# An encoder layer: head 0 of the dilated attention prepared beside two dense groups instead of one, and three loads of output weights tied to later heads

## The chip, the cores and the metric

The kernel runs on one core of a Trainium2 chip. The metric is the device time of one execution in microseconds (us). Five engines matter here: TensorE (PE, matrix products; PEld is its weight load), VectorE (DVE), ScalarE (ACT), GpSimd (POOL) and SyncE (SP), which issues most DMAs. Each works through its own queue in order, and they wait for each other by semaphores.

## The reference, cut to what matters

One encoder layer over 1024 positions of width 1024, in float32:

```
proj = rms_norm(x) @ w_in                       # qA kA vA qB kB vB
out_a = dense attention, 8 query heads on 2 key/value heads, QK-norm and axial rotary
out_b = 8 heads: three dilated windows (128,1), (512,4), (2048,16), ALiBi distance penalty,
        merged by their softmax denominators
x = x + concat(rms_norm(out_a), rms_norm(out_b)) @ w_out
x = x + (gelu(gate) * value) @ w_down           # gate, value: depthwise conv of rms_norm(x) @ w_up
```

## The kernel before

The program is one straight sequence of instructions. Its stages are the input projection, the dense attention, the dilated attention, the output projection, the up-projection with convolution and gate, and the down-projection. All large operands live in two arenas on chip, `bigf` (plain float32) and `bigr` (operands of products), addressed by fixed offsets, so that buffers of different stages share places. PSUM (`ps`) is used as eight banks of 512 columns. Most products are made of three: a value is split into a rounded copy (an ACT copy) and the rest (a DVE or POOL subtraction), and high*high, high*low and low*high are added.

**Order.** The Python code issues the steps in program order, but a scheduler then orders each engine's queue by the data dependences; an instruction whose operands are free early can be put well ahead of where the code has it. Lists of small steps (`prep`) are taken a few at a time between the steps of the main loops, by `take`.

**Dense attention** (loop from L1037): 16 groups `g`, each four query heads of one block of 128 queries. `a_main` runs over 8 key tiles `kt`: two score products (L624, L625) into bank 2 or 3, an exponential on ACT (L627), and two tiles later the product with the values (`pv`, L619, four matmuls of 65 columns). After each tile it takes `plan[kt]` steps of `prep`. `a_prep(g + 1)` has seven: `nat` (split of the queries), `first` (four transposes, copy L592), four `mx` (score products L597 and a row maximum L598), `last` (transposes, copy L605). With the plan (1, 1, 1, 1, 1, 1, 1, 0) group g prepares group g + 1. Group 15 has no successor. It takes the 16 steps for head 0 of the dilated attention instead, by the plan (3, 2, 2, 2, 2, 2, 2, 1).

**Dilated attention** (loop from L1077): 8 heads `h`, each 8 steps `s`. `b_s` makes a bias product (L747), score products (L759 and L761 for s < 4, L769 and L770 behind), and an exponential (L773). For s < 4 the result is then split (ACT copy L775, DVE subtraction L776), for the others it is multiplied by a count on DVE (L778). Two steps later `b_pv` multiplies with the values (L790, L795) and collects in `F_OS` (L798 on ACT, L802 on DVE); `b_out` transposes back (L807) and normalises (L639, L640). While a head runs, the next one is prepared: `b_split` (copies L675 and L576, subtractions on POOL) and the 15 steps of `b_prep`:

- `trq`: four transposes (L177) and the ACT copy L700; `trk`: four transposes, ACT copies L691 and L692, DVE casts L693 and L694;
- `mx`, eight times: products into banks 0 and 1 (L707, L708, L711, L712), each followed by a DVE row maximum (L718);
- `trl`: a DVE maximum (L726), four transposes, ACT copy L731, whose result the scores L761 need.

In the same list stands `b_split(h + 1)`, so head 1 is split inside the preparation of head 0.

**Output weights.** `w_out` is loaded in eight parts of 512 KB (`wo_load`, L812) and split (`wo_split`: ACT L818, DVE L819). A table gives the head and step after which each is issued:

```
wo_early = {(4, 0): [(wo_load, 0)], (4, 5): [(wo_split, 0), (wo_load, 1)], (5, 5): [(wo_split, 1), (wo_load, 2)], ...
F_WOR = [O_F + o for o in (2560, 2560, 2560, 3584, 5632, 6656, 2560, 5632)]
```

Parts 0, 1 and 2 go through the same place, where the dense attention keeps its values until its last group. Nothing in the data ties load 0 to head 4. Parts 5 to 7 are split behind the last head.

Of the kernel before, what the change touches and what calls it, by code (L numbers as in the profile page):

```python
# [83 lines left out]
F_OS = O_F + 1536  # L84
# [14 lines left out]
F_WOR = [O_F + o for o in (2560, 2560, 2560, 3584, 5632, 6656, 2560, 5632)]  # L99
# [24 lines left out]
def tile_encoder_layer(ctx, tc, x, w_in, gains, outg, norm1_g, norm2_g, w_out, w_up, conv_w, conv_b,  # L124
# [15 lines left out]
    vec = nc.vector  # L140
# [4 lines left out]
    def f(off, n):  # L145
        return bigf[:, off:off + n]
# [62 lines left out]
    def qab(tt):  # L209
        return O_QAB + 1024 * tt  # L210
# [362 lines left out]
    def q_nat(src, stride, eng, n, o, qln=R_QLN):  # L573

        q = fp(src, [stride, n], [1, 64])
        act(rp(R_QD + o, [128, n], [64, 2], [1, 64]), fp(src, [stride, n], [0, 2], [1, 64]), AF.Copy)  # L576
        eng.tensor_tensor(rp(qln + o, [128, n], [1, 64]), q, rfp(R_QD + o, [128, n], [1, 64]), op=OP.subtract)


    def a_prep(g):  # L580
        b, kv = divmod(g, 2)
        q2 = R_Q2A + 512 * (g % 2)
        ql = R_QLA + 512 * (g % 2)

        def nat():
            q_nat(qab(b) + 256 * kv, 64, vec, 4, 512 * kv)

        def first():
            t = next_tr()
            for i in range(4):  # L590
                tr_r(t, i, r(R_QD + 128 * (4 * kv + i), 128))
            act(r(q2, 512), bank(t), AF.Copy)  # L592

        def mx(i):
            for hf in range(2):
                b = hf
                mm(bank(b), r(q2 + 128 * i, 128), r(R_K2A + 1024 * kv + 512 * hf, 512), start=True, stop=True)  # L597
                vec.tensor_reduce(f(SM_MC + 8 * hf + i, 1), bank(b), axis=AX.X, op=OP.max)  # L598

        def last():  # L600
            vec.tensor_tensor(rp(R_QLN + 512 * kv + 64, [128, 4]), f(SM_MC, 4), f(SM_MC + 8, 4), op=OP.max)
            t = next_tr()
            for i in range(4):
                tr_r(t, i, r(R_QLN + 128 * (4 * kv + i), 128))
            act(r(ql, 512), bank(t), AF.Copy)  # L605

        return [nat, first] + [lambda i=i: mx(i) for i in range(4)] + [last]

    def a_main(g, prep, tail, late, plan, late_plan):

        b, kv = divmod(g, 2)
        q2 = R_Q2A + 512 * (g % 2)
        ql = R_QLA + 512 * (g % 2)
        ob = 6 + g % 2
        slots = {}

        def pv(kt):
            for i in range(4):
                mm(bank(ob, 65, 66 * i), f(slots[kt] + 128 * i, 128), f(F_VA + 132 * kt + 66 * kv, 65),  # L619
                   start=(kt == 0 and i == 0), stop=(kt == 7), skip_group_check=True)  # L620

        for kt in range(8):
            st = 2 + kt % 2
            mm(bank(st), r(R_K2A + 1024 * kv + 128 * kt, 128), r(q2, 512), start=True, stop=False)  # L624
            mm(bank(st), r(R_KHA + 1024 * kv + 128 * kt, 128), r(ql, 512), start=False, stop=True)  # L625
            slots[kt] = p_slots()[0]
            act(f(slots[kt], 512), bank(st), AF.Exp)  # L627
            take(prep, plan[kt])
            take(late, late_plan[kt])
            if tail and kt in (0, 1, 2):  # L630
                tail.pop(0)()
            if kt >= 2:
                pv(kt - 2)

        return [lambda: pv(6), lambda: pv(7), lambda: o_norm(ob, 66, qab(b) + 256 * kv, ([64, 4], [1, 64]))]
# [37 lines left out]
    def b_split(h):  # L673
        k3 = fp(F_KN[h % 2], [64, 8], [1, 64])
        act(rp(R_KN, [128, 8], [1, 64]), k3, AF.Copy)  # L675
        gp.tensor_tensor(rp(R_KN + 64, [128, 8], [1, 64]), k3, rfp(R_KN, [128, 8], [1, 64]), op=OP.subtract)
        q_nat(O_QAB + 512 + 64 * h, 1024, gp, 8, 0, R_QLB[h % 2])
        if h < 6:
            load_k(h + 2)

    def b_prep(h):
        k2n, k2c, khn, khc, q2c, qlc = sets(h)

        def trk(hf):

            t = next_tr()
            for i in range(4):
                tr_r(t, i, r(R_KN + 128 * (4 * hf + i), 128))
            nat = pp(512 * t, [256, 2], [32, 8], [1, 32])
            to = lambda o: rp(o + 64 * hf, [32, 2], [128, 8], [1, 32])  # L690
            act(r(k2c + 512 * hf, 512), bank(t), AF.Copy)  # L691
            act(to(k2n), nat, AF.Copy)  # L692
            vec.tensor_copy(r(khc + 512 * hf, 512)[0:64], bank(t)[0:64])  # L693
            vec.tensor_copy(to(khn)[0:64], nat[0:64])  # L694

        def trq(hf):
            t = next_tr()
            for i in range(4):
                tr_r(t, i, r(R_QD + 128 * (4 * hf + i), 128))
            act(r(q2c + 512 * hf, 512), bank(t), AF.Copy)  # L700

        def mx(tt):
            rr, c = divmod(tt, 2)
            q = r(q2c + 128 * tt, 128)
            m0 = k2c + 112 * c
            if rr % 3:
                mm(bank(0, 144 * rr), q, rp(m0, [256, rr], [1, 144]), start=True, stop=True)  # L707
                mm(bank(0, 432 - 144 * rr, 144 * rr), q, rp(m0 + 256 * (rr + 1), [256, 3 - rr], [1, 144]),  # L708
                   start=True, stop=True)
            else:  # L710
                mm(bank(0, 432), q, rp(m0 + (256 if rr == 0 else 0), [256, 3], [1, 144]), start=True, stop=True)  # L711
            mm(bank(1, 256), q, r(k2c + 256 * rr, 256), start=True, stop=True)  # L712
            tmx = F_TMX[h % 2]
            for i, (ps, tab, n) in enumerate((
                    (bank(0, 432), fp(tmx + 384 + 160 * (3 - rr) + 16 * (1 - c), [160, 3], [1, 144]), 432),
                    (bank(1, 256), f(tmx + 128 * (1 - c), 256), 256))):
                junk = f(F_JK2[i], n // 2).bitcast(BF)
                vec.tensor_tensor_reduce(out=heads(junk, 3) if i == 0 else junk, in0=heads(ps, 3) if i == 0 else ps,  # L718
                                         in1=tab, scale=1.0, scalar=-3e38, op0=OP.add, op1=OP.max,
                                         accum_out=f(SM_MC + 8 * i + tt, 1))  # L720
            if tt == 7 and h < 6:
                load_tmx(h + 2)

        def trl(hf):
            qln = R_QLB[h % 2]
            vec.tensor_tensor(rp(qln + 64 + 512 * hf, [128, 4]), f(SM_MC + 4 * hf, 4), f(SM_MC + 8 + 4 * hf, 4),  # L726
                              op=OP.max)
            t = next_tr()
            for i in range(4):
                tr_r(t, i, r(qln + 128 * (4 * hf + i), 128))  # L730
            act(r(qlc + 512 * hf, 512), bank(t), AF.Copy)  # L731

        L = lambda fn, a: (lambda: fn(a))
        return [L(trq, 0), L(trk, 0), L(trk, 1), L(mx, 0), L(trq, 1), L(mx, 1), L(mx, 2),
                L(mx, 3), L(trl, 0), L(mx, 4), L(mx, 5),
                L(b_split, h + 1) if h < 7 else None, L(mx, 6), L(mx, 7), L(trl, 1)]
# [199 lines left out]
    prep = [lambda: fill(rp(R_QLN + 64, [128, 8], [1, 64]), 8, 64, 0.0)] + a_prep(0)  # L936
# [90 lines left out]
    late = last_sums + [t for d in deferred[:2] for t in done(*d, 0)[3:]]  # L1027
# [6 lines left out]
    load_tabs(1)  # L1034

    tail = []
    for g in range(16):  # L1037
        prep = a_prep(g + 1) if g < 15 else [lambda: b_split(0)] + b_prep(0)
        tail = a_main(g, prep, tail, late, (3, 2, 2, 2, 2, 2, 2, 1) if g == 15 else (1, 1, 1, 1, 1, 1, 1, 0),
                      (0, 1, 1, 0, 1, 0, 1, 0) if g < 3 else (0, 0, 1, 0, 1, 0, 1, 0) if g < 7 else (0, 1, 0, 0, 0, 1, 0, 0))  # L1040
        if g == 7:
            dma(f(F_CNT, 384), cnt)
            gp.memset(fp(F_VCN + 64, [66, 8]), 1.0)
            load_vc(0)
        if g == 11:
            load_k(0)
            load_k(1)
        if g == 5:
            v_split(R_VB, F_VBN)
            load_v(1)  # L1050
        take(fills, 1)
# [8 lines left out]

    def mixer_out_early(h, s):
        for fn, k in wo_early.get((h, s), []):
            fn(k)
        if h != 7:
            return
        if s in (0, 2):
            mix_tr(s // 2, 0)
        if s in (1, 3):
            mix_sq(s // 2, 0)
        if s == 4:  # L1070
            dma(f(F_G2, 1024), bcast(norm2_g, 1024))
        if s == 7:
            proj_out(0, 0, 0)
            proj_out(0, 0, 1)

    lag = 2
    for gs in range(64 + lag + 1):  # L1077
        h, s = divmod(gs, 8)
        if s == 0:
            prep = b_prep(h + 1) if h < 7 else []  # L1080
# [375 lines left out]
```

## Time and profile before

| | |
|---|---|
| median of 3 runs | 1342.73 us (1342.39 to 1345.34) |
| profiled execution | 1343.92 us, its span 1342.2 us |
| mean granted TensorE clock | 0.999 |
| ACT busy, DVE busy, POOL busy | 674.0, 991.7, 363.4 us |
| dense groups, PE | first score product at 211.5, last value product at 431.3 us |
| head 0, first bias product | 431.3 us |
| last bias product of head 7 | 590.5 us |
| w_out loads issued | 431.57, 437.99, 449.64, 554.71 us, four more from 573.09 to 582.04 |

All times inside the execution are counted from the start of the span. A row of the order of time gives start, duration, engine, line and operation, and in brackets how long the engine idled before it and whose end released it. L-numbers are lines of the kernel before.

### The profile page before, as it was taken

How to read it: one execution, taken by the hardware profiler on the slowest of the kernel's cores; microseconds unless marked ns; L12 is line 12 of the kernel's file. 1: busy time of each engine (PE TensorE's matmuls, PEld its weight loads, DVE VectorE, ACT ScalarE, POOL GpSimd, SP SyncE). 2: the span in 40 equal slices, each digit the busy share in tenths (PEclk: the TensorE clock that was granted, in tenths of full speed). 3: DMA queues.
4: the chain of work that ended last, by engine and by line, in shares of the span. 5: the costliest groups of instructions: out<-in, count | busy, mean ns of one | idle time of the engine just before them, and what ended most of it. 6: DMA issues, size and time to landing. Idle time of an engine off the chain costs nothing.

```text
span 1342.2 us, 20068 instructions
## 1 busy us (share of the span) xinstructions
PE 1311.1 (98%) x7559; PEld 1134.9 (85%) x7559; DVE 991.7 (74%) x1613; ACT 674.0 (50%) x1057; POOL 363.4 (27%) x274
## 2 busy tenths in 40 slices
PE   8999999999999999999999999999999999999998
PEld 7999989989998888878877788888888888888887
DVE  4987696864545888876579877887787789586664
ACT  7855553644445776764365444444444445244331
POOL 1611123020001222100114565556656651100000
PEclk9999999999999999999999999999999999999999
DMA  7144212000001333252222233232233325897873
GB/s 256 53 123 114 80 39 65 9 9 0 1 1 34 107 105 81 67 166 79 94 87 71 102 110 111 86 102 96 102 115 105 102 101 190 283 311 228 293 223 113
DMA packets 119859, 148.08 MB, mean 110 GB/s; under 512 B 50833, under 2 KB 76881, under 8 KB 119761
## 3 DMA queue, kind: packets, MB, share of 16 engines
q1 hardware_dynamic: 118609, 143.65, 33.3%
q0 software_dynamic: 1152, 3.15, 0.9%
q8 instruction: 59, 0.97, 0.3%
q14 instruction: 39, 0.32, 0.1%
HBM read 112.95 MB, written 33.82 MB: 109 GB/s over the span
## 4 chain that ended last, share of the span: by engine, by line
PE 70%; DVE 16%; ACT 5%; issue 4%; POOL 4%; DMA 1%; SPq 0%; DVEq 0%; ACTq 0%; POOLq 0%
PE ps L619 7%; PE ps L1161 7%; PE ps L1162 7%; PE ps L1163 7%; PE ps L1277 5%; PE ps L1276 5%; PE ps L1278 5%; DVE bigf L1194 4%; PE ps L624 2%; PE ps L597 2%; PE ps L625 2%; POOL bigf L1208 2%; PE ps L862 2%; PE ps L795 2%; PE ps L864 2%
## 5 line engine op out<-in xcount | busy, mean ns | idle before, releaser
L1161 PE MATMUL ps<-bigr 128*128 128x512 f32 x616 | 241.1, 392 | 6.6 <-DVE bigf L1165 6.1
L1162 PE MATMUL ps<-bigr 128*128 128x512 f32 x616 | 239.8, 389 | 0.0
L1163 PE MATMUL ps<-bigr 128*128 128x512 f32 x616 | 239.7, 389 | 0.0
L1144 ACT ACTIVATE bigr<-bigf 128x512 fp32r<-128x512 f32 x154 | 92.8, 624 | 159.2 <-POOL bigf L1136 95.4
L1194 DVE SCALAR_TENSOR_TENSOR bigf<-bigf 128x768 f32<-128x768 f32 (+1 forms) x176 | 146.4, 889 | 26.3 <-ACT bigf L1192 26.3
L619 PEld LDWEIGHTS ps<-bigf 128*128 128x128 f32 x1024 | 139.4, 191 | 10.5
L1161 PEld LDWEIGHTS ps<-bigr 128*128 128x128 f32 x616 | 115.6, 188 | 35.6 <-DVE bigf L1165 9.9
L1145 DVE TENSOR_TENSOR bigr<-bigf,bigr 128x512 fp32r<-128x512 f32 x112 | 116.5, 1057 | 32.6 <-ACT bigr L1144 32.6
L1256 ACT ACTIVATE bigr<-bigf 128x1024 fp32r<-128x1024 f32 x77 | 80.6, 1059 | 119.5 <-PE ps L1278 76.9
L1163 PEld LDWEIGHTS ps<-bigr 128*128 128x128 f32 x616 | 115.6, 188 | 24.2
L1162 PEld LDWEIGHTS ps<-bigr 128*128 128x128 f32 x616 | 115.6, 188 | 23.6
L619 PE MATMUL ps<-bigf 128*128 128x65 f32 x1024 | 134.3, 267 | 0.0
L405 PE MATMUL ps<-bigr 128*128 128x256 f32 x448 | 127.2, 284 | 1.2 <-ACT bigf L291 1.2
L406 PE MATMUL ps<-bigr 128*128 128x256 f32 x448 | 126.8, 283 | 0.0
L407 PE MATMUL ps<-bigr 128*128 128x256 f32 x448 | 126.7, 283 | 0.0
L627 ACT ACTIVATE bigf<-ps 128x512 f32<-128x512 f32 x128 | 75.7, 597 | 93.5 <-PE ps L625 91.1
L1277 PE MATMUL ps<-bigr 128*128 128x512 f32 x308 | 119.9, 389 | 0.0
L1278 PE MATMUL ps<-bigr 128*128 128x512 f32 x308 | 119.8, 389 | 0.0
L1276 PE MATMUL ps<-bigr 128*128 128x512 f32 x308 | 119.8, 389 | 0.0
L1257 DVE TENSOR_TENSOR bigr<-bigf,bigr 128x1024 fp32r<-128x1024 f32 x77 | 93.0, 1221 | 28.7 <-ACT bigr L1256 26.7
L598 DVE TENSOR_REDUCE bigf<-ps 128x1 f32<-128x512 f32 x128 | 86.0, 689 | 23.6 <-PE ps L597 22.2
L1208 POOL TENSOR_TENSOR bigf<-bigf 128x512 f32<-128x512 f32 x44 | 69.1, 1590 | 89.9 <-DVE bigf L1199 65.6
(221 smaller groups left out, 2892.6 us busy)
## 6 DMA issues: line engine op xcount, KB each, us to landing
bigf<-w_down SPq DMA_DIRECT2D x99, 256.0 KB, 4.3
bigf<-w_up SPq DMA_DIRECT2D x44, 512.0 KB, 4.2
bigf<-gscr SPq DMA_DIRECT2D x77, 256.0 KB, 4.1
gscr<-bigf SPq DMA_DIRECT2D x33, 512.0 KB, 2.7
bigf<-w_in SPq DMA_DIRECT2D x8, 1024.0 KB, 5.3
bigf<-x SPq DMA_DIRECT2D x15, 512.0 KB, 6.6
bigf<-tmx SPq DMA_DIRECT2D x8, 672.0 KB, 5.1
bigf<-w_out SPq DMA_DIRECT2D x8, 512.0 KB, 4.0
```

Source lines behind the costliest of these rows:

```text
L405: mm(o, ah, wh, start=(k == 0 and t % 2 == 0 and n != 2), stop=False, skip_group_check=True)
L406: mm(o, ah, wl, start=False, stop=False, skip_group_check=True)
L407: mm(o, al, wh, start=False, stop=(k == 3), skip_group_check=True)
L619: mm(bank(ob, 65, 66 * i), f(slots[kt] + 128 * i, 128), f(F_VA + 132 * kt + 66 * kv, 65), start=(kt == 0 and i == 0), stop=(kt == 7), skip ...
L1145: (gp if n in (2, 4) and m > 3 else vec).tensor_tensor(rp(o + 512, [128, 4], [1, 128]), src, rfp(o, [128, 4], [1, 128]), op=OP.subtract)
L1161: mm(bank(b), wh, th, start=(k == 0 and n in (1, 5, 6, 7)), stop=False, skip_group_check=True)
L1162: mm(bank(b), wh, tl, start=False, stop=False, skip_group_check=True)
L1163: mm(bank(b), wl, th, start=False, stop=(k == 3), skip_group_check=True)
L1194: vec.scalar_tensor_tensor(f(a + o, n), f(i + d, n), w_, f(a + o, n), op0=OP.mult, op1=OP.add)
L1276: mm(o, ah, r(d, 512), start=(q == 0 and n in (1, 5, 2)), stop=False, skip_group_check=True)
L1277: mm(o, ah, r(d + 1024, 512), start=False, stop=False, skip_group_check=True)
L1278: mm(o, al, r(d, 512), start=False, stop=(q == NQ - 1), skip_group_check=True)
```

## The change

The list `prep` now lives across groups. Group 14 gets the steps of `a_prep(15)` and, behind them, those of head 0; it takes 11 steps by the plan (1, 1, 1, 1, 1, 2, 2, 2), so the last four (`b_split(0)`, `trq(0)`, both `trk`) are of head 0. Group 15 takes the other 12 by (2, 2, 2, 2, 1, 1, 1, 1). And for heads below 6 (loads 0, 1 and 2) a DVE copy of one column from `F_OS` into the first column of the load's place is put ahead of the load. `F_OS` is written by the head before, so the copy, and the load that overwrites it, can't be ordered ahead of that.

```
     tail = []
+    prep = []
     for g in range(16):
-        prep = a_prep(g + 1) if g < 15 else [lambda: b_split(0)] + b_prep(0)
-        tail = a_main(g, prep, tail, late, (3, 2, 2, 2, 2, 2, 2, 1) if g == 15 else (1, 1, 1, 1, 1, 1, 1, 0),
+        prep += a_prep(g + 1) if g < 15 else []
+        if g == 14:
+            prep += [lambda: b_split(0)] + b_prep(0)
+        tail = a_main(g, prep, tail, late, {14: (1, 1, 1, 1, 1, 2, 2, 2), 15: (2, 2, 2, 2, 1, 1, 1, 1)}.get(
+            g, (1, 1, 1, 1, 1, 1, 1, 0)),
...
         for fn, k in wo_early.get((h, s), []):
+            if fn is wo_load and h < 6:
+                vec.tensor_copy(f(F_WOR[k], 1), f(F_OS, 1))
             fn(k)
```

## The prediction

> **What bounds the kernel now.** I read the page's busy times first, then the busy time of each engine in stretches of one dilated head, then the order of time of single engines around the change.
>
> ```profile
> PE 1311.1 (98%) x7559; PEld 1134.9 (85%) x7559; DVE 991.7 (74%) x1613; ACT 674.0 (50%) x1057; POOL 363.4 (27%) x274
> ```
>
> The stretches give, after their bounds and length, busy time and (instructions) of each engine, then the granted clock and the DMA columns.
>
> ```profile
> core 0: us, PE busy (x) PEld busy (x) DVE busy (x) ACT busy (x) POOL busy (x), PEclk, DMA share, GB/s
> 391.40:404.80 13.40, 13.40 (x97) 12.30 (x97) 6.15 (x12) 6.29 (x11) 0.00 (x0) 1.00 0.00 1
> 431.30:451.50 20.20, 17.18 (x117) 15.43 (x116) 16.39 (x49) 15.08 (x26) 2.81 (x3) 0.92 0.39 111
> 491.50:511.50 20.00, 19.51 (x141) 16.95 (x139) 17.09 (x54) 13.72 (x25) 3.74 (x4) 1.00 0.37 94
> 511.50:531.80 20.30, 20.00 (x142) 17.01 (x141) 16.47 (x51) 13.73 (x25) 4.98 (x5) 1.00 0.31 81
> 552.20:572.40 20.20, 19.90 (x142) 16.92 (x140) 16.27 (x51) 14.31 (x25) 1.83 (x3) 1.00 0.27 72
> ```
>
> TensorE (PE) is busy for 98% of the span, so a change gains only what PE now idles or runs slowly. A dense group (the 391.40 row) leaves it no idle time, and the later dilated heads leave 0.3 to 0.5 us in 20. Head 0 is the exception: 3.0 us of 20.2 idle, and a mean granted clock of 0.92. PE's own order of time says where (start, duration, instruction; in brackets the idle time before it and what ended it):
>
> ```profile
> 432.10 0.46 PE L177 MATMUL ps<-bigr 128*128 128x128 f32 x4
> 432.40 0.48 PE L747 MATMUL ps<-bigr 128*128 128x512 f32 x1
> 432.71 0.28 PE L759 MATMUL ps<-bigr 128*128 128x256 f32 x1
> 433.34 0.84 PE L177 MATMUL ps<-bigr 128*128 128x128 f32 x8 [0.35 <-ACT bigr L700]
> 435.02 0.39 PE L761 MATMUL ps<-bigr 128*128 128x256 f32 x1 [0.84 <-ACT bigr L731]
> ...
> 437.55 0.73 PE L711 MATMUL ps<-bigr 128*128 128x432 f32 x1 [1.19 <-ACT bigr L691]
> ...
> 439.56 0.41 PE L761 MATMUL ps<-bigr 128*128 128x256 f32 x1
> ...
> 441.68 0.48 PE L747 MATMUL ps<-bigr 128*128 128x256 f32 x2
> 442.00 0.28 PE L759 MATMUL ps<-bigr 128*128 128x256 f32 x1
> ...
> 446.64 0.37 PE L707 MATMUL ps<-bigr 128*128 128x288 f32 x1 [0.62 <-DVE bigf L718]
> ```
>
> The brackets add to 0.35 + 0.84 + 1.19 + 0.62 = 3.0 us, three of the four waits being for ScalarE (ACT). Behind the third, the same product takes 0.41 us instead of 0.28. Two stretches show why:
>
> ```profile
> 433.00:437.40 4.40, 2.18 (x18) 1.87 (x18) 2.22 (x5) 3.71 (x8) 0.00 (x0) 1.00 0.80 249
> 437.40:440.80 3.40, 3.25 (x12) 2.99 (x13) 3.23 (x6) 2.94 (x7) 1.23 (x1) 0.50 0.48 151
> ```
>
> After a stretch in which PE was busy 2.18 of 4.40 us, the granted clock is 0.50 for 3.4 us. The 3.25 us of work there would have taken half at full clock: 1.6 us lost. So the place holds 3.0 + 1.6 = **4.6 us** in all, and no more can be gained.
>
> **The change part by part.** What ACT and VectorE (DVE) did in that place:
>
> ```profile
> 433.89 0.60 ACT L691 ACTIVATE bigr<-ps 128x512 fp32r<-128x512 f32 x1 [0.69 <-PE ps L177]
> 434.38 0.59 ACT L731 ACTIVATE bigr<-ps 128x512 fp32r<-128x512 f32 x1
> 434.86 0.60 ACT L692 ACTIVATE bigr<-ps 128x512 fp32r<-128x512 f32 x1
> 435.33 1.16 ACT L818 ACTIVATE bigr<-bigf 128x1024 fp32r<-128x1024 f32 x1
> 436.38 0.61 ACT L773 ACTIVATE ps<-ps 128x512 f32<-128x512 f32 x1
> 436.89 0.61 ACT L691 ACTIVATE bigr<-ps 128x512 fp32r<-128x512 f32 x1
> ```
> ```profile
> 436.70 1.27 DVE L819 SCALAR_TENSOR_TENSOR bigr<-bigf,bigr 128x1024 fp32r<-128x1024 f32 x1
> 438.01 0.69 DVE L776 TENSOR_TENSOR bigr<-ps,bigr 128x512 fp32r<-128x512 f32 x1
> 438.62 0.67 DVE L693 CAST bigr<-ps 64x512 fp32r<-64x512 f32 x1
> 439.22 0.67 DVE L694 CAST bigr<-ps 64x512 fp32r<-64x512 f32 x1
> ```
>
> The copy L731, on which head 0's first scores wait (the 0.84), stands behind a copy L691 of head 1. The first split of output weights (L818 on ACT, 1.05 us to the next start; L819 on DVE, 1.27) stands ahead of the first exponential L773 and the second L691, and L711 waits 1.19 us for that L691.
>
> *Preparation spread over groups 14 and 15.* The steps are the same 15, and with group 15's own seven and the split of head 0 they make 23 calls: 11 in group 14, 12 in group 15. Nothing is added. In the built program most of the row-maximum products of head 0 stand one key tile of group 15 earlier; its last four transposes now stand ahead of the first scores that use them, and L731 ahead of L700 and L691. In group 14's last tile four copies of 0.48 us stand on ACT between two exponentials, so one comes about 2.5 us after the last instead of the usual 1.7 (13.40 for eight tiles). Worked along PE's new order, that is hidden behind the eight transposes and the value products but for about 0.1 us: **+0.1** (from 0 to 0.8, the whole lateness).
>
> *Loads held back.* Before, SyncE's queue had w_out load 0 ahead of other loads:
>
> ```profile
> 431.57 0.35 SPq L812 DMA_DIRECT2D bigf<-w_out  x1
> 432.94 0.35 SPq L660 DMA_DIRECT2D bigf<-tmx  x1
> ```
>
> Load 0 waited for the end of the dense groups' values, with head 2's table behind it; nobody on PE waited for that table. In the changed program load 0 stands behind head 6's table, loads 1 and 2 about a head apart, so I cost the transfers themselves at nothing: each has a later split as its only reader, and if one came late, that split would wait, not PE. What matters is that splits 0 and 1 leave head 0 and land in heads 4 and 5.
>
> *What is late next in head 0.* Up to 432.99 PE has no gap, so I count from there. In the new order the last four transposes of head 0 and the first four of head 1 are issued together, at T; of the work that stood ahead of 433.0, the four L177, L747 and L759 from 432.10 to 432.83 (0.73 us by starts) come behind T, so T is about 432.26. L731 starts 0.5 us later (as L700 did, at 432.60 after transposes at 432.10), ACT copies follow each 0.48 us. The first scores end at T + 1.5, their exponential starts at T + 1.7, L691 at T + 2.2, the copy L775 at T + 2.7, ending at T + 3.3. L712 can start when L691 has ended, at T + 2.8; DVE then does its short row maximum, L776 from T + 3.6, four casts, and the second L776 from T + 6.6, at 0.60 us each (438.01, 438.62, 439.22). The second one frees the bank for the bias L747 that stood at 441.68: T + 7.3. PE has 8.34 (433.34 to 441.68) - 0.84 - 1.19 - 1.6 + 0.73 + 0.12 (one product moved forward) = 5.56 us of work until then, so 1.74 us is idle in place of 2.38 + 1.6 = 3.98: 2.24 gained. The fourth wait of 0.62 goes too: it is for DVE, whose queue has lost the 1.27 us of L819. **-2.8 us** (2.86, from 0 to -4.6).
>
> The new idle time could drop the clock again. In before, 2.2 us of idle time in 4.4 did. In my walk PE waits 0.13 for L731, 0.35 for L691, 0.35 for L775 and 0.6 for row maximum and L776, some 1.4 us between T + 1.1 and T + 4.3, and 0.3 before the fourth bias. The Trainium skill ("TensorE: Matmul & The Clock Gate", Part 1: The HAM clock gate) has the clock halved after an idle window of some 3.4 us and asks only that single gaps stay below that. The trace agrees on 0.50 and on 3.4 us as its length, but its longest gap before the drop is 1.19. By the skill's rule the new gaps could not do it and the sum stays; by the row they might, and the sum loses 1.6.
>
> *Splits in heads 4 and 5.* Two kinds of row bound them.
>
> ```profile
> 448.30 1.28 DVE L819 SCALAR_TENSOR_TENSOR bigr<-bigf,bigr 128x1024 fp32r<-128x1024 f32 x1
> ```
> ```profile
> 447.00:455.00 8.00, 7.97 (x59) 6.96 (x57) 7.75 (x24) 3.86 (x7) 1.83 (x2) 1.00 0.40 110
> ```
> ```profile
> 563.10 1.15 ACT L818 ACTIVATE bigr<-bigf 128x1024 fp32r<-128x1024 f32 x1 [0.19 <-PE ps L759]
> ```
> ```profile
> 525.37 0.59 DVE L718 CUSTOM_DVE_ANT_1 bigf<-ps,bigf 128x432 bf16<-128x432 f32 x1
> ```
> ```profile
> 526.03 0.33 PE L707 MATMUL ps<-bigr 128*128 128x144 f32 x1
> ```
> ```profile
> L726 DVE TENSOR_TENSOR bigr<-bigf 128x4 fp32r<-128x4 f32 x2 | 0.3, 160 | 0.0
> ```
>
> For nothing: the split at 448.30 stands in a stretch where DVE is busy 7.75 of 8.00, and PE idles 0.03; head 6 carries ACT's L818 at 563.10 and idles 0.3. Against: in head 4 the built order puts L819 just before the row maximum that ran at 525.37 to 525.90, and PE's L707 followed at 526.03 in the same bank, with 0.13 us to spare. Pushed by up to 1.27, it stalls PE by up to 1.1. Queued behind L819 are that row maximum and L776, for which the value products wait. PE's built order in both heads has other work moved ahead of these, so I take under half, 0.45 for each: **+0.9** (from 0 to 2.5). The three copies of one element cost DVE 0.16 each by the L726 row and are inside that. Split 2 stays in head 6 on ACT.
>
> **Sum:** -2.8 + 0.9 + 0.1 = -1.8 us. The profiled execution took 1343.92 (span 1342.2 and 1.7 around it), 1.2 above the median of the three runs; from the median, 1342.73 - 1.8 = **1340.9 us**.
>
> **The rivals.**
> - *Everything is recovered.* If ACT and DVE run ahead and the splits hide as at 448.30, only some 0.8 us of new gaps stay: -4.6 + 0.8 = -3.8, 1338.9. For it: the 7.97 of 8.00. Against: DVE's six passes of 0.60 us between the first scores and the fourth bias, which the change does not shorten.
> - *The clock drops anyway.* Head 0 still idles some 1.7 us and then runs 3.4 us at 0.50: -1.8 + 1.6 = -0.2, 1342.5. For it: no single gap above 1.19 was needed. Against: the other boundaries idle up to 0.5 us with the clock at 1.00 (the 491.50 row).
> - *Slower: the splits stall DVE in heads 4 and 5 and drop the clock there.* Each costs its 1.27 and 1.6 of slow clock, 2.87; twice that less 2.8 is +2.9: 1345.6. It decides from the point where PE's idle time in some 4 us reaches about 2, as at 433.00. For it: 0.13 us of slack at 526.03. Against: both heads are 98% busy.
> - That the change does not do what it says is out: the built order shows both moves.
>
> **How the numbers follow.** Forecast 0.46, full recovery 0.30, clock drop 0.12, slower 0.12. A measurement of this kernel tells about 0.2% (2.7 us) from no change. The forecast lies inside it, with 0.06 of its chance beyond the faster edge, as 0.9 of cost may be nothing; the clock drop lies inside. Faster 0.30 + 0.06 = 0.36, same 0.40 + 0.12 = 0.52, slower 0.12. The range goes from the whole 4.6 gained, 1338.1, less half a microsecond for the runs' own spread, to the clock drop with another 1.6 us of split cost, 1344.1: 1337.6 to 1344.1. It leaves out the slower case and little else.
>
> **What would show it.** Right: the granted clock at 1.00 from 430 to 450; no L818 or L819 between 430 and 510; the four waits above gone, and in their place short ones for L775, L691 and L776 adding to 1.5 to 2 us; PE idle in heads 4 and 5 up by 0.3 to 0.6 each, ended by L718 or L776. Wrong: a clock below 1.00 anywhere from 430 to 600; PE idle in the last two dense groups above 0.5 us; heads 4 and 5 unchanged or over 1 us longer; any difference in length behind 600, where each engine's built order is the same.

## The result and the profile after

The changed kernel takes 1347.53 us (median of 20 runs, 1344.62 to 1349.68) where the kernel before, run beside it, takes 1343.93 (20 runs, 1342.36 to 1346.10): a ratio of 1.0024, 95% interval 1.0018 to 1.0030; the medians lie 3.6 us apart. The forecast was 1340.9 us in a range of 1337.6 to 1344.1; the time lies above the range. Of the 6.6 us between forecast and time, 1.2 are the base: the prediction counted from the 1342.73 of three runs, and the twenty runs beside give 1343.93. The profiled execution after took 1347.56 us (span 1345.8).

Where in the program the time arose is read from the starts of the same products in both traces. First the kernel before: the first score product of the dense groups (from a view of one line: least, median and longest duration in ns, then first and last start), the first bias product of heads 4 and 7, and the first product of the up-projection (from PE's order of time).

```profile
L624 PE MATMUL ps<-bigr x128: 389/476/499, 211.6 to 426.7; 128*128 128x512 f32 x128
```
```profile
513.28 0.59 PE L747 MATMUL ps<-bigr 128*128 128x256 f32 x2
...
574.16 0.59 PE L747 MATMUL ps<-bigr 128*128 128x256 f32 x2
...
696.92 0.48 PE L1161 MATMUL ps<-bigr 128*128 128x512 f32 x1
```

The same of the kernel after, whose lines behind 1068 are 8 higher:

```profile
L624 PE MATMUL ps<-bigr x128: 389/476/497, 212.5 to 428.7; 128*128 128x512 f32 x128
```
```profile
512.11 0.59 PE L747 MATMUL ps<-bigr 128*128 128x256 f32 x2
...
574.78 0.47 PE L747 MATMUL ps<-bigr 128*128 128x256 f32 x1
...
700.71 0.48 PE L1169 MATMUL ps<-bigr 128*128 128x512 f32 x1
```

After stands 0.9 us later at the first score product, 1.17 earlier at head 4, 0.62 later at head 7 and 3.79 later at the up-projection; from there on the distance stays (3.83 at its six hundredth product). The first 0.9 lies ahead of anything that the change touches (0.7 of it is there at the first product of the input projection, 28.22 against 27.54) and differs between executions, so it is taken off. Then the dense groups and heads 0 to 3 **gained 2.1 us**, heads 4 to 6 **lost 1.8**, and head 7 with the output projection **lost 3.2**.

The page of after has nearly the same busy times as before's:

```profile
PE 1311.8 (97%) x7559; PEld 1135.0 (84%) x7559; DVE 991.6 (74%) x1616; ACT 674.3 (50%) x1057; POOL 363.1 (27%) x274
```

The work is the same; DVE has three instructions more, the copies of one element. What differs is idle time, and the stretches show it. Those of the prediction, now of the kernel after, and two more:

```profile
core 0: us, PE busy (x) PEld busy (x) DVE busy (x) ACT busy (x) POOL busy (x), PEclk, DMA share, GB/s
391.40:404.80 13.40, 13.40 (x98) 12.30 (x98) 6.17 (x11) 5.73 (x11) 0.00 (x0) 1.00 0.00 1
431.30:451.50 20.20, 18.70 (x133) 16.32 (x132) 15.36 (x51) 13.13 (x24) 3.74 (x3) 1.00 0.17 49
511.50:531.80 20.30, 19.03 (x138) 16.47 (x137) 17.48 (x54) 14.38 (x26) 4.07 (x4) 1.00 0.36 107
531.80:552.20 20.40, 19.47 (x139) 16.43 (x138) 17.59 (x54) 14.57 (x26) 3.37 (x4) 1.00 0.37 105
572.40:592.00 19.60, 15.88 (x101) 13.32 (x100) 13.27 (x27) 12.52 (x22) 1.18 (x1) 0.91 0.47 149
```

And of the kernel before, the two that the prediction did not show:

```profile
531.80:552.20 20.40, 19.91 (x143) 17.21 (x141) 17.49 (x57) 13.72 (x25) 3.98 (x5) 1.00 0.30 80
572.40:592.00 19.60, 18.52 (x126) 15.61 (x125) 14.70 (x30) 14.20 (x25) 0.66 (x1) 1.00 0.48 149
```

Head 0 has its clock of 1.00 and PE is busy 18.70 us there instead of 17.18; the dense group is as full as it was. Heads 4 and 5 each idle more. Head 7, of which the prediction says nothing, lost 2.64 us of PE's busy time, and its mean clock fell to 0.91. What happened there, first in ACT's order of time after:

```profile
576.69 0.60 ACT L731 ACTIVATE bigr<-ps 128x512 fp32r<-128x512 f32 x1 [0.42 <-PE ps L177]
579.83 1.15 ACT L818 ACTIVATE bigr<-bigf 128x1024 fp32r<-128x1024 f32 x1 [2.54 <-DMA bigf<-w_out]
580.88 0.58 ACT L773 ACTIVATE ps<-ps 128x512 f32<-128x512 f32 x1
581.40 0.58 ACT L203 ACTIVATE bigr<-ps 128x512 fp32r<-128x512 f32 x1
```

then in PE's:

```profile
582.03 0.79 PE L862 MATMUL ps<-bigr 128*128 128x512 f32 x1 [2.60 <-ACT bigr L203]
582.62 0.63 PE L863 MATMUL ps<-bigr 128*128 128x512 f32 x1
```

The instruction in front of head 7's first exponential (L773) is the ACT copy of a split of output weights, and it waits 2.54 us for its load. Behind it in ACT's queue stand the exponential and L203, the copy that the first product of the output projection (L862) reads; PE waits 2.60 us for that. The load was issued at 574.27:

```profile
574.27 0.33 SPq L812 DMA_DIRECT2D bigf<-w_out  x1
```

Before, the same load was issued at 574.03. Its last piece landed at 579.15 before and at 579.75 after, 0.60 later, and head 7 itself starts 0.62 later: the load is not what moved. The split stood elsewhere. ACT and PE before:

```profile
577.57 0.58 ACT L773 ACTIVATE ps<-ps 128x512 f32<-128x512 f32 x1 [0.91 <-PE ps L761]
578.06 0.59 ACT L203 ACTIVATE bigr<-ps 128x512 fp32r<-128x512 f32 x1
...
579.02 0.62 ACT L773 ACTIVATE ps<-ps 128x512 f32<-128x512 f32 x1
579.53 1.16 ACT L818 ACTIVATE bigr<-bigf 128x1024 fp32r<-128x1024 f32 x1
```
```profile
578.71 0.50 PE L862 MATMUL ps<-bigr 128*128 128x512 f32 x1
579.05 0.40 PE L863 MATMUL ps<-bigr 128*128 128x512 f32 x1
```

There two exponentials pass first, the split finds its data landed 0.4 us earlier, and nobody waits. This is the fifth split (part 4). The table in the code asks for it after step 5 of head 7; the scheduler had moved it up, before to behind the second exponential of head 7, after to ahead of the first. Neither edit names it.

Near the end of the wait the clock halves, for 3.4 us; PE's L863 takes 0.63 us instead of 0.40:

```profile
581.57:584.98 3.41, 2.95 (x10) 2.48 (x11) 3.21 (x5) 1.97 (x4) 0.00 (x0) 0.50 0.79 231
```

### The profile page after: what moved, and what is told of

It reads as the page before. It is cut to its first block, busy times and chain, and to the rows that moved or that the text cites. A ratio compares the mean times of both kernels' runs of the same rounds, so it can differ in the third digit from the quotient of the medians.

```text
span 1345.8 us, 20065 instructions
## 1 busy us (share of the span) xinstructions
PE 1311.8 (97%) x7559; PEld 1135.0 (84%) x7559; DVE 991.6 (74%) x1616; ACT 674.3 (50%) x1057; POOL 363.1 (27%) x274
## 4 chain that ended last, share of the span: by engine, by line
PE 74%; DVE 14%; ACT 4%; issue 3%; POOL 2%; DMA 2%; SPq 0%; ACTq 0%; DVEq 0%; POOLq 0%
PE ps L1169 8%; PE ps L1170 8%; PE ps L1171 8%; PE ps L619 7%; PE ps L1286 5%; PE ps L1285 5%; PE ps L1284 5%; PE ps L624 2%; PE ps L597 2%; PE ps L625 2%; DVE bigf L1202 2%; PE ps L862 2%; PE ps L405 2%; PE ps L406 2%; PE ps L863 2%
## 5 line engine op out<-in xcount | busy, mean ns | idle before, releaser
L405 PE MATMUL ps<-bigr 128*128 128x256 f32 x448 | 127.2, 284 | 1.2 <-ACT bigf L291 1.2
L407 PE MATMUL ps<-bigr 128*128 128x256 f32 x448 | 126.7, 283 | 0.0
```

Source lines behind the costliest of these rows:

```text
L405: mm(o, ah, wh, start=(k == 0 and t % 2 == 0 and n != 2), stop=False, skip_group_check=True)
L407: mm(o, al, wh, start=False, stop=(k == 3), skip_group_check=True)
```

## The experiments

Theory: the loss is the fifth split, which waits for its load in front of ACT's queue; the rest of the change gains. Rivals: the held loads or the splits in heads 4 and 5 cost it, or it comes with the later loads. Eleven runs. The table gives, for the profiled execution of each, how much later (+) it stood than before at the first dense score product ("start"), and what was lost (+) or gained from there to head 4, in heads 4 to 6, and from head 7 to the up-projection, each worked from the starts of the same products as above; then where behind 431 the clock was 0.50, and the ratio with its interval. The kernel before was run beside each on the same chip (medians 1343.97, 1344.16 and 1344.06). Two pairs are one kernel profiled twice, e3 with e10 and e5 with e11: they agree within 0.1 us to head 4 and in heads 4 to 6, and within 0.5 and 0.8 from head 7 on, so that column is good to no more than that.

| kernel | start | to head 4 | heads 4-6 | head 7 on | clock 0.50 at | median, ratio |
|---|---|---|---|---|---|---|
| after | +0.9 | -2.1 | +1.8 | +3.2 | 581.6-585.0 | 1347.53, 1.0024 (1.0018-1.0030) |
| e1_spread_only | +1.2 | -1.6 | +0.7 | +5.4 | 581.3-588.2 | 1347.61, 1.0023 (1.0012-1.0035) |
| e2_hold_only | +0.3 | -1.0 | +1.8 | +2.3 | none | 1349.27, 1.0038 (1.0026-1.0050) |
| e3_split4_held | +0.3 | -2.0 | +1.8 | -0.8 | none | 1343.48, 0.9996 (0.9987-1.0004) |
| e4_load4_held | +0.3 | -2.0 | +1.8 | +0.6 | none | 1344.56, 1.0007 (0.9999-1.0016) |
| e5_spread_split4_held | +0.8 | -1.5 | +0.7 | -0.9 | none | 1343.05, 0.9990 (0.9981-0.9999) |
| e6_before_split4_held | 0.0 | +0.3 | 0.0 | -0.3 | 439.2-442.6 | 1344.25, 1.0002 (0.9993-1.0010) |
| e7_pool_splits01 | +1.5 | -1.9 | +4.7 | -0.1 | 530.3-533.7 | 1347.73, 1.0029 (1.0016-1.0041) |
| e8_no_splits01 | +1.1 | -1.9 | +0.7 | -0.9 | none | 1342.81, 0.9990 (0.9981-0.9999) |
| e9_hold_split4 | +1.1 | -0.3 | +1.8 | -0.1 | 438.7-442.1 | 1344.81, 1.0005 (0.9996-1.0014) |
| e10_split4_again | +1.2 | -2.1 | +1.8 | -0.3 | none | 1343.43, 0.9994 (0.9985-1.0003) |
| e11_spread_split4_again | +0.2 | -1.6 | +0.7 | -0.2 | none | 1342.86, 0.9991 (0.9982-1.0000) |

**e1_spread_only.** The changed kernel without the held loads:

```
-            if fn is wo_load and h < 6:
-                vec.tensor_copy(f(F_WOR[k], 1), f(F_OS, 1))
             fn(k)
```

> Only the preparation is spread over groups 14 and 15; the loads of the output weights are not held, so splits 0 and 1 come in heads 0 and 1. In the built order the fifth split (part 4) stands ahead of head 7's first exponential, as in the changed kernel. Theory A (the loss is that fifth split, whose ACT copy waits for its load ahead of the exponential: 2.5 us idle and 1.5 us of halved clock behind it): still slower than before or level with it, about +1.5 us, since the gain in head 0 is smaller than 2.2 with a split still there and the loss of 3.4 in head 7 stays; PE waits over 2 us for L203 near 580. Theory B (the loss is splits 0 and 1 in heads 4 and 5): faster than before by about 1.5 us.

It is as slow as the whole change, and slower than the 1.5 us expected. Its executions reach from 1344.17 to 1349.46, so the loss differs between them, and the trace, of 1349.36, shows one of the longest. ACT's order and PE's wait in it:

```profile
580.03 1.15 ACT L818 ACTIVATE bigr<-bigf 128x1024 fp32r<-128x1024 f32 x1 [3.13 <-DMA bigf<-w_out]
```
```profile
582.23 0.80 PE L862 MATMUL ps<-bigr 128*128 128x512 f32 x1 [3.17 <-ACT bigr L203]
```

So the held loads do not cause the wait; the spread preparation alone displaces the fifth split as well. That PE's wait is as long as ACT's, within 0.1 us, speaks for the queue.

**e2_hold_only.** The kernel before with those two lines, and the preparation as it was.

> Only the three loads are held; head 0 is prepared in group 15 alone, as before. The fifth split stands ahead of head 7's first exponential here too. Theory A: +3 us against before (1 to 1.5 gained in head 0 by the missing split, 1.3 lost in heads 4 and 5, 3.4 lost in head 7). Theory B: about level, +0 to +0.5 us, with no long wait near 580.

This has the slowest median of all. Each half of the change displaces the fifth split for itself:

```profile
582.49 0.50 PE L862 MATMUL ps<-bigr 128*128 128x512 f32 x1 [2.60 <-ACT bigr L203]
```
```profile
572.40:592.00 19.60, 15.87 (x112) 13.46 (x111) 13.63 (x27) 13.32 (x24) 1.28 (x1) 1.00 0.48 149
```

The same wait as after, of 2.60 us, but here the clock stays at 1.00 in this execution. This one took 1347.10 us, at a mean clock of 1.000; the other four took 1348.68 to 1350.51, at 0.997. So the median holds drops of the clock that this trace does not show, and lies 5.3 us above before where 3 were expected.

**e3_split4_held.** The changed kernel, in which the weight of the fifth split's scaling (`O_OG + 4`) gets zero times a column of `F_OS` added, so that the split can't be ordered ahead of the ACT copy (L798) that writes this column in head 7. In its trace that copy starts at 586.03 and the split at 587.03:

```
+            if fn is wo_split and k == 4:
+                vec.scalar_tensor_tensor(f(O_OG + 4, 1), f(F_OS, 1), 0.0, f(O_OG + 4, 1), op0=OP.mult, op1=OP.add)
             fn(k)
```

> The changed kernel, with one more DVE operation of one column (the scale of part 4 plus zero times a column of the collected output) that ties split 4 to head 7's fifth step; in the built order its ACT copy then stands behind head 7's third exponential. Theory A: the wait of 2.6 us for L203 near 580 and the halved clock behind it go, 3 to 3.5 us faster than the changed kernel: level with before within 0.5 us. Theory B: within 1 us of the changed kernel, so +2.5 to +3.5 us against before.

One DVE instruction on one column takes the loss away: 1343.48 against 1347.53, and the executions, from 1343.09 to 1344.25, no longer spread over 5 us as after's do (1344.62 to 1349.68). The ACT copies of head 7 stand as before, and the stretch of head 7 is whole:

```profile
577.44 0.58 ACT L773 ACTIVATE ps<-ps 128x512 f32<-128x512 f32 x1 [0.71 <-PE ps L761]
...
578.54 0.59 ACT L203 ACTIVATE bigr<-ps 128x512 fp32r<-128x512 f32 x1
```
```profile
572.40:592.00 19.60, 18.48 (x126) 15.57 (x125) 14.96 (x29) 14.41 (x25) 0.62 (x1) 1.00 0.47 143
```

**e4_load4_held.** The changed kernel with the hold put on the fifth load too, instead of on its split:

```
-            if fn is wo_load and h < 6:
+            if fn is wo_load and (h < 6 or k == 4):
```

> The changed kernel, with load 4 held like loads 0 to 2 by a DVE copy of one column from the collected output; the fifth split then stands behind head 7's third exponential in the built order. Theory A: as with split 4 held, level with before within 0.7 us. Theory B: +2.5 to +3.5 us against before.

The split moves back behind other exponentials, but its load is now the late one, and the same wait is seen smaller, at another place:

```profile
584.91 1.15 ACT L818 ACTIVATE bigr<-bigf 128x1024 fp32r<-128x1024 f32 x1 [0.84 <-DMA bigf<-w_out]
585.97 0.58 ACT L775 ACTIVATE bigr<-ps 128x512 fp32r<-128x512 f32 x1
```
```profile
586.60 0.51 PE L790 MATMUL ps<-bigr 128*128 128x256 f32 x2 [1.32 <-ACT bigr L775]
```

ACT's wait for the load and the loss behind head 7's start thus go together: 3.13, 2.54 and 2.55 us (e1, after, e2) with +5.4, +3.2 and +2.3, 0.84 (e4) with +0.6, none (e3) with -0.8. Waits alike with unlike losses, as in after and e2, differ in the clock.

**e5_spread_split4_held and e6_before_split4_held.** The edit of e3 on the spread alone (e1) and on the kernel before.

> Preparation spread, loads not held, split 4 tied to head 7's fifth step. If the three terms add (spread alone 1.6 us gained up to head 4, 0.7 lost in heads 4 to 6, 0.8 gained in head 7 with the fifth split out of the way): 1.7 us faster than before. If the fifth split was the whole loss and holding the loads costs nothing: the same as the changed kernel with split 4 held, 0.5 us faster than before.

> The kernel before with only split 4 tied to head 7's fifth step. In before the fifth split stands behind head 7's second exponential and finds its load landed. Theory A: only the 0.8 us of head 7 seen with split 4 held, so 0.5 to 1 us faster than before. If tying it were a gain of its own of 4 us: 1340.

On the kernel before the edit is worth nothing (1.0002, where 0.5 to 1 us of gain was expected), so e3 shows the loss undone and not a gain of the edit's own. The spread with it is faster than the kernel before by about 1 us, between the 0.5 and 1.7 of its expectation.

**e7_pool_splits01.** e3, with the scaling and the subtraction of splits 0 and 1 on POOL, to take their 1.27 us each off DVE in heads 4 and 5:

```
+        if k < 2:
+            gp.tensor_scalar(raw, raw, g, None, op0=OP.mult)
+            act(r(R_WO[k], 1024), raw, AF.Copy)
+            gp.tensor_tensor(r(R_WO[k] + 1024, 1024), raw, rf(R_WO[k], 1024), op=OP.subtract)
+            return
```

> The changed kernel with split 4 held; in splits 0 and 1 the weights are scaled and the rest is subtracted on POOL, DVE's two operations of 1.27 us go. If DVE's queue in heads 4 and 5 is what costs 1.8 us there: 1 us faster than with split 4 held alone, 1.5 us faster than before. If ACT's copies or the order cost it: no change from split 4 held.

Slower, where a gain was expected, by the same mechanism in another place. The copy (here L820) waits for POOL's 2.84 us scaling (here L819) in ACT's queue, and the copy L775 behind it feeds DVE, whose queue PE then waits for; behind that the clock halves (the table's 530.3). POOL, ACT, DVE and PE:

```profile
523.07 2.84 POOL L819 TENSOR_SCALAR bigf<-bigf 128x1024 f32<-128x1024 f32 x1
```
```profile
525.95 1.06 ACT L820 ACTIVATE bigr<-bigf 128x1024 fp32r<-128x1024 f32 x1 [2.33 <-POOL bigf L819]
526.91 0.58 ACT L775 ACTIVATE bigr<-ps 128x512 fp32r<-128x512 f32 x1
```
```profile
527.52 0.69 DVE L776 TENSOR_TENSOR bigr<-ps,bigr 128x512 fp32r<-128x512 f32 x1 [1.62 <-ACT bigr L775]
```
```profile
528.79 0.40 PE L707 MATMUL ps<-bigr 128*128 128x288 f32 x1 [1.99 <-DVE bigf L718]
```

**e8_no_splits01.** e3 with splits 0 and 1 left out of the table `wo_early`, so that two eighths of the output projection's weights are never prepared; the time is read for what those splits cost.

> The changed kernel with split 4 held and with splits 0 and 1 left out altogether (parts 0 and 1 of the output weights are not prepared). It prices both splits in heads 4 and 5: by the two profiles so far 1.1 us (1.8 lost there with them, 0.7 without), so 1.1 us faster than split 4 held alone. By the forecast's own term 0.9; if they cost nothing, no difference.

Heads 4 to 6 lose 0.7 us instead of 1.8, so the two splits cost 1.1 us net there: 1.4 in heads 4 and 5, less 0.3 that came back in head 6.

**e9, e10 and e11.** On one chip, with the fifth split held in each: the hold alone (e2 with the split held), both parts (e3 again) and the spread alone (e5 again).

> The hold alone, on the preparation of before, with the fifth split held behind the second exponential. My theory (the displaced fifth split was the whole loss; the two moved splits cost about 1.1 in heads 4 and 5; head 0 gains about 1.0 from losing its split): no wait over 0.3 us at the first L862 of head 7, ratio about 0.9997 (0.999 to 1.0005). If the hold itself is what costs time: slower, ratio 1.002 or more.

> Both parts of the change with the fifth split held, beside the other two kernels of this call on one chip. My theory: ratio about 0.9993 (0.9985 to 1.0), no loss from the hold beyond the 1.1 of the two splits, and faster than the hold alone by about 1 us. Rival (the spread gives nothing): equal to the hold alone.

> The spread preparation alone, no hold, with the fifth split held. My theory: ratio about 0.9993 (0.9983 to 1.0), within half a microsecond of both parts together, since the splits left in heads 0 and 1 cost there about what the held ones cost in heads 4 and 5. Rival (the hold is worth its own gain): over 1 us slower than both parts together.

The hold alone gains nothing that its interval shows (1.0005, 0.9996 to 1.0014). The expectation put its head 0 at a gain of 1.0, as in e2; here it is 0.3, since the clock halved in head 0 in this execution. The spread alone and both parts together lie 0.6 us apart, which their intervals do not tell apart; in the traces the hold gains 0.5 in the transition and loses 1.1 in heads 4 to 6. What gains, by the medians, is the spread: the fastest complete version is the spread without the hold, with the fifth split kept back. It measured 0.9990 and 0.9991 of before on two chips, about 1 us, with intervals that end at 0.9999 and 1.0000.

## Why the prediction was wrong, point by point

**The step that failed** is the one on the loads: "I cost the transfers themselves at nothing: each has a later split as its only reader, and if one came late, that split would wait, not PE." The split waits in ACT's queue, and what stands behind it waits too: 2.54 us on ACT became 2.60 on PE, and 3.2 us from head 7 on. The step also looked at loads 0 to 2 alone. The load that was waited for is the fifth, which the change does not touch. It landed no later against head 7's start than before; its reader came earlier: ACT came to it at 577.29, and before at 579.53. The sum of the prediction has no term for head 7, since I followed the order of the queues only in the places where the diff puts something, and took the rest for the same. Why the scheduler moves this one split when either half of the change is made is not settled: the runs show that each half does it and that a dependence prevents it.

**Preparation spread, +0.1.** The dense groups stay full: 13.40 of 13.40 us in the 391.40 row, before and after. Head 0 starts 0.2 us later than before, beyond the start's difference, with more of its preparation done.

**Head 0, -2.8.** The mechanism was right and the size too large. The clock is 1.00 from 430 to 450, the four waits are gone, and no split is there. Up to the fourth bias the short waits of the walk came, but shorter: 0.12 us for L691 and 0.10 for L775 instead of 0.35 each, and 0.22 and 0.39 for L776. The last of these rows stands behind it:

```profile
437.38 0.50 PE L747 MATMUL ps<-bigr 128*128 128x512 f32 x1 [0.22 <-DVE bigr L776]
...
440.36 0.50 PE L747 MATMUL ps<-bigr 128*128 128x256 f32 x2 [0.39 <-DVE bigr L776]
...
443.06 0.39 PE L712 MATMUL ps<-bigr 128*128 128x256 f32 x1 [0.29 <-DVE bigf L718]
```

The starts tell which term of the -2.86 was mis-sized. Head 0's first bias product starts at 431.35 before and 432.48 after, the bias product of its fourth step at 441.68 and 440.36. Up to there 2.45 us were gained, of which about 0.3 is a row-maximum product (L711) that now stands elsewhere: the 2.24 was right. The other term, "The fourth wait of 0.62 goes too", failed. From that bias product to the first of head 1, after took 0.38 us longer instead of 0.62 less. The wait of 0.62 is gone, but others, of 0.15, 0.29 and 0.18, stand in its place, and a few transposes more (some 0.2). Head 1's first bias product, before and then after:

```profile
453.47 0.59 PE L747 MATMUL ps<-bigr 128*128 128x256 f32 x2
```
```profile
452.53 0.59 PE L747 MATMUL ps<-bigr 128*128 128x256 f32 x2
```

So head 0 lasted 22.12 us before and 20.05 after, 2.07 less, and e3 and e10 repeat it (20.08 and 20.06). The bound of 4.6 us was too high as well. Heads 3 to 6 of before take 20.33 us on the mean for products of 31,624 columns in all; head 0 has 29,744, which at that pace is about 19.1 us. By this estimate some 3.0 us were to be had, and 2.07 were.

**Splits in heads 4 and 5, +0.9.** The place was right: the wait in front of the L707 that the prediction shows at 526.03, for the row maximum behind L819. After:

```profile
525.90 0.33 PE L707 MATMUL ps<-bigr 128*128 128x144 f32 x1 [0.77 <-DVE bigf L718]
```

The size was 1.4 for the two splits (e8), inside the range of 0 to 2.5. To it come 0.4 us in head 6, which I had at nothing; the whole is +1.8 in heads 4 to 6. Of that, 0.7 goes with the spread alone (e5, e11) and without the splits (e8); its cause was not looked for further.

**The sum.** Without the wait in head 7, -2.1 + 1.8 - 0.5 (the mean of that column in e3 and e10) makes -0.8, and those two runs measured 0.5 and 0.6 us under before: no difference that the measurement can tell, as the forecast had it, but a third of its gain of 1.8.

**The rivals.** The slower case named splits that stall PE and then drop the clock, and its 2.87 us each is near what one stall cost; but it had them on DVE in heads 4 and 5, where the clock stayed at 1.00, and not on ACT in head 7. "A clock below 1.00 anywhere from 430 to 600" was the sign named, and it is there, at 581.6.

**The clock.** I made the drop in head 0 a fixed price of that place, of 1.6 us. With short waits it is not fixed. In e2 and e9 head 0 has the same code and the same three waits for ACT (0.35, 0.83 and 0.46 us in the one, 0.35, 0.84 and 0.46 in the other). In e2 the clock stays at 1.00 behind them, and in e9 it is halved. The stretch behind the waits in each, e2 first:

```profile
437.40:440.80 3.40, 3.08 (x21) 2.36 (x21) 3.19 (x7) 3.02 (x7) 1.31 (x1) 1.00 0.00 0
```
```profile
438.70:442.10 3.40, 3.33 (x13) 2.61 (x13) 3.12 (x8) 2.34 (x6) 1.28 (x1) 0.50 0.00 0
```

From its first bias product to head 1's, head 0 lasts 21.32 us in e2 and 22.04 in e9: there the drop cost 0.7 us, less than half of the 1.6. With the longer wait of before (1.19 us in front of L711) no trace shows head 0 without a drop: before and e6 both have one. And none of the 81 executions of before beside the experiments has a mean clock of 1.000, which a single drop excludes (half of 3.4 us in 1342 is 0.0013); of the 65 of e3, e4, e5, e8, e10 and e11, whose head 0 has no drop in the trace, 22 have. So in before the drop may well have come each time; that is not shown.

The Trainium skill ("TensorE: Matmul & The Clock Gate", Part 1: The HAM clock gate) says that the window over which activity is judged is free-running, and that it depends on where in the window the first matmul lands when the clock changes. Two executions with the same waits and different clocks in mid-kernel fit that. Its rule to have no idle gaps over some 3.4 us is not enough here: the clock fell in e9's head 0, where no single wait is above 0.84.

## What to carry to other kernels

An instruction that waits for a transfer costs what stands behind it in its engine's queue, so "its only reader is not urgent" is no reason for nothing: look at which instruction is next. Where a scheduler sets the order, compare the whole order of each engine's queue before and after, above all the few instructions that wait for a DMA, also far from the edit; a dependence of one column (e3) is enough to hold one back. And read what a stretch can give from start to start, against a steady stretch of the same work; idle time plus slow clock came out too high here (4.6 us against some 3.0).

## What the runs showed of the hardware

- The same wait of 2.60 us in front of L862 went with 3.4 us of half clock (after) or none (e2), and one of 3.17 with twice that (e1):

```profile
581.30:588.20 6.90, 5.97 (x22) 5.32 (x23) 4.37 (x6) 3.88 (x8) 0.00 (x0) 0.51 0.39 123
```

- The same is seen far from the change. Near 190 us, among the last products of the input projection (L405 to L407), PE waits 1.7 to 2.1 us for ACT in every one of these kernels; in seven of the eleven experiments the clock is 0.50 for 3.4 us behind it, in the other four experiments, in before and in after it stays at 1.00. Two executions of one and the same kernel (the spread with the fifth split held), first e5, then e11:

```profile
187.60:191.10 3.50, 1.47 (x15) 1.33 (x14) 3.50 (x5) 3.50 (x6) 0.00 (x0) 1.00 0.00 0
191.10:194.50 3.40, 3.40 (x31) 3.40 (x30) 3.40 (x5) 3.38 (x7) 0.03 (x1) 1.00 0.02 5
```
```profile
187.60:191.10 3.50, 1.67 (x16) 1.57 (x15) 3.50 (x5) 3.50 (x7) 0.00 (x0) 1.00 0.02 5
191.10:194.50 3.40, 3.40 (x18) 3.40 (x18) 3.40 (x5) 3.38 (x6) 0.69 (x1) 0.51 0.00 0
```
